# Gather, running sum and matmul on one core: casts moved from ScalarE into the gathers, single-tile drains, and an unrolled TensorE program

## The chip, the core and the metric

The kernel runs on one core of one Trainium2 chip. The metric is the device time of one execution in microseconds (us). Executions were timed in rounds, each kernel beside the kernel before on the same chip. "TensorE", "VectorE", "ScalarE" and "GpSimd" stand in the profile as PE (with PEld for the loading of weights), DVE, ACT and POOL; SP is SyncE, which here only issues loads and stores.

## The reference

```python
B, S, N, D = 16, 4096, 2048, 512
# x: (16, 4096, 512) f32; indices: (16, 2048) int64, sorted, no repeats; w: (512, 512) f32
gathered = x[np.arange(B)[:, None], indices, :]
out = np.matmul(np.cumsum(gathered, axis=1), w)        # (16, 2048, 512) f32
```

32,768 rows of 2 KB are fetched (67 MB) and as many rows of 2 KB are written (67 MB). The kernel works in 256 tiles of 128 rows. Two tiles make a group.

## The kernel before

For every tile GpSimd issues one indirect DMA that fetches 128 rows of f32. ScalarE casts a group to fp16. TensorE multiplies the tile with a triangular matrix, which gives the running sums inside the tile, already transposed (L149, `pa`). VectorE adds the last column of the tile before and writes fp16 (`cst`). TensorE multiplies with `w` (L185, `pb`). ScalarE copies the product of a group out of PSUM in one go, and SyncE stores it.

```python
def gather(t):                       # GpSimd
    g, r = divmod(t, R)              # R = 2 tiles in a group
    if g >= NG // R:                 # NG = 16 tiles in flight
        pool.need(s_c0, R)
        pool.need(s_c, g - NG // R)  # buffer free when the cast of 8 groups ago is done
    ...
    nc.gpsimd.indirect_dma_start(out=g32[g % (NG // R)][:, r, :], in_=x_flat, ...)

def cast(g):                         # ScalarE, three groups ahead of its drain
    for t in range(R * g, R * g + R):
        act.need(s_g[t % NG], 16 * (t // NG + 1))
    act.need(s_a, R * (g - NH + 1))
    nc.scalar.copy(out=g16[g % NH][:], in_=g32[g % (NG // R)][:]).then_inc(s_c, 1)

def drain(g):                        # ScalarE
    act.need(s_o[g % NO], 16 * (g // NO))
    act.need(s_b, R * (g + 1))
    nc.scalar.copy(out=ob[g % NO][:], in_=pb[g % NB][:]).then_inc(s_e, 1)
...
# TensorE: the middle of its program is a loop whose waits compare with a register
with nc.tensor.Fori(LOOP, G - LOOP, LOOP) as first:
    for g in range(LOOP):
        step(g, first)               # project(g, j), then sums of two groups ahead
```

Of the kernel before, what the change touches and what calls it, by code (L numbers as in the profile page):

```python
# [7 lines left out]
P = 128  # L8
FP32 = mybir.dt.float32
FP16 = mybir.dt.float16  # L10
# [17 lines left out]
def kernel(  # L28
# [7 lines left out]
    nc = tc.nc  # L36

    B, S, D = x.shape
    N = indices.shape[1]
    R = 2  # L40
    Q = P // R
    DC = D // P
    NT = N // P
    T = B * NT
    G = T // R
# [1 line left out]
    KI = T // P  # L47
    FIRST = 2 * R
    NG = 16
    NH = 4  # L50
    NA = 4
    NB = 2
    NC = 4
    NO = 8
    LOOP = 4
    AH = 2
    assert D == 512 and N % (R * P) == 0 and T % P == 0

# [2 lines left out]
    const = ctx.enter_context(tc.tile_pool(name="const", bufs=1))  # L61
    ps = ctx.enter_context(tc.tile_pool(name="ps", bufs=1, space=bass.MemoryType.PSUM))
# [3 lines left out]
    idxf = const.tile([P, KI, P], FP32)  # L66
    idxg = const.tile([P, KI, P], U32)
# [3 lines left out]
    ident = const.tile([P, P], FP32)  # L71
    zeros = const.tile([P, D], FP16)
    spare = const.tile([P, 1], FP16)
    g32 = [const.tile([P, R, D], FP32, name=f"g32_{i}") for i in range(NG // R)]
    g16 = [const.tile([P, R, D], FP16, name=f"g16_{i}") for i in range(NH)]
    cst = [const.tile([P, DC, R, P], FP16, name=f"cst{i}") for i in range(NC)]
    ob = [const.tile([P, R, D], FP32, name=f"ob{i}") for i in range(NO)]
    pa = [ps.tile([P, DC, R, Q], FP32, name=f"pa{i}") for i in range(NA)]
    pb = [ps.tile([P, R, D], FP32, name=f"pb{i}") for i in range(NB)]

    ctx.enter_context(tc.tile_critical(no_gpsimd_drain=True))  # L81

    def sem(name):
        return tc.alloc_semaphore(name)

    s_z, s_ut, s_wc, s_if, s_pt, s_prep, s_c0, s_c1 = (
        sem(f"s_{n}") for n in ("z", "ut", "wc", "if", "pt", "prep", "c0", "c1")
    )
# [3 lines left out]
    s_el = [sem(f"s_el{j}") for j in range(R)]  # L92
    s_ol = [sem(f"s_ol{j}") for j in range(R)]
    s_g = [sem(f"s_g{i}") for i in range(NG)]
    s_o = [sem(f"s_o{i}") for i in range(NO)]
    s_c = sem("s_c")
    s_a = sem("s_a")
    s_d = sem("s_d")
    s_b = sem("s_b")
    s_e = sem("s_e")  # L100

    pool, pe, dve, act, sp = (
        Lane(e) for e in (nc.gpsimd, nc.tensor, nc.vector, nc.scalar, nc.sync)
    )

    def gather(t):
        g, r = divmod(t, R)
        if g >= NG // R:
            pool.need(s_c0, R)
            pool.need(s_c, g - NG // R)  # L110
        if t < FIRST:
            pool.need(s_first[g], 16)
            ap = idx_first[:, t, 0:1]
        else:
            pool.need(s_prep, t // P + 1)
            ap = idxg[:, t // P, t % P : t % P + 1]
        nc.gpsimd.indirect_dma_start(  # L117
            out=g32[g % (NG // R)][:, r, :],
            out_offset=None,
            in_=x_flat,  # L120
            in_offset=bass.IndirectOffsetOnAxis(ap=ap, axis=0),
            element_offset=(t // NT) * S * D,
        ).then_inc(s_g[t % NG], 16)

    def cast(g):
        for t in range(R * g, R * g + R):
            act.need(s_g[t % NG], 16 * (t // NG + 1))
        act.need(s_a, R * (g - NH + 1))
        nc.scalar.copy(out=g16[g % NH][:], in_=g32[g % (NG // R)][:]).then_inc(s_c, 1)  # L129

    def cast_tile(t, done):
        g, r = divmod(t, R)
        act.need(s_g[t % NG], 16 * (t // NG + 1))
        act.need(s_a, R * (g - NH + 1))
        nc.scalar.copy(out=g16[g % NH][:, r], in_=g32[g % (NG // R)][:, r]).then_inc(done, 1)  # L135

    def sums(t, first=0):
        g, r = divmod(t, R)
        if isinstance(first, int):
            if g in (0, G - 1):  # L140
                pe.need(s_c1 if g else s_c0, r + 1)
            else:
                pe.need(s_c, g)
            pe.need(s_ut, 4)
            pe.need(s_d, t - NA + 1)
        elif r == 0:
            nc.tensor.wait_ge(s_c, first + g)
        for c in range(DC):
            mm = nc.tensor.matmul(  # L149
                out=pa[t % NA][:, c],  # L150
                lhsT=g16[g % NH][:, r, c * P : (c + 1) * P],
                rhs=ut[:],
                start=(c == 0),
                stop=(c == DC - 1),
            )
        mm.then_inc(s_a, 1)

    def carry(t):
        g, r = divmod(t, R)
        dve.need(s_b, R * (g - NC + 1))  # L160
        dve.need(s_a, t + 1)
        dst = cst[g % NC][:, :, :, r * Q : (r + 1) * Q]
        if t % NT == 0:
            nc.vector.tensor_copy(out=dst, in_=pa[t % NA][:]).then_inc(s_d, 1)  # L164
            return
        e = (r - 1) % R
        last = cst[(t - 1) // R % NC][:, :, R - 1, e * Q + Q - 1 : e * Q + Q]
        dve.need(s_d, t)
        nc.vector.tensor_tensor(  # L169
            out=dst,  # L170
            in0=pa[t % NA][:],
            in1=last.unsqueeze(2).broadcast_to([P, DC, R, Q]),
            op=mybir.AluOpType.add,
        ).then_inc(s_d, 1)

    def project(g, j, first=0):
        if isinstance(first, int):
            pe.need(s_wc, DC)
            pe.need(s_d, R * (g + 1))
            pe.need(s_e, g - NB + 1)  # L180
        elif j == 0:
            nc.tensor.wait_ge(s_d, R * first + R * (g + 1))
            nc.tensor.wait_ge(s_e, first + (g - NB + 1))
        for c in range(DC):
            mm = nc.tensor.matmul(  # L185
                out=pb[g % NB][:, j],
                lhsT=cst[g % NC][:, c, j, :],
                rhs=w16[:, c, :],
                start=(c == 0),
                stop=(c == DC - 1),  # L190
            )
        mm.then_inc(s_b, 1)

    def drain(g):
        act.need(s_o[g % NO], 16 * (g // NO))
        act.need(s_b, R * (g + 1))
        nc.scalar.copy(out=ob[g % NO][:], in_=pb[g % NB][:]).then_inc(s_e, 1)  # L197

    def store(g):
        b, h = divmod(g, GB)  # L200
        dst = out[b, h * R * P : (h + 1) * R * P, :].rearrange("(p j) d -> p j d", j=R)
        sp.need(s_e, g + 1)
        nc.sync.dma_start(out=dst, in_=ob[g % NO][:]).then_inc(s_o[g % NO], 16)

    def drain_last(j, lane, copy):
        g = G - 1
        lane.need(s_o[g % NO], 16 * (g // NO))
        lane.need(s_b, R * g + j + 1)
        copy(out=ob[g % NO][:, j], in_=pb[g % NB][:, j]).then_inc(s_el[j], 1)  # L209

    def store_last():
        b, h = divmod(G - 1, GB)
# [6 lines left out]
    with nc.allow_non_contiguous_dma(reason="a few indices, one per partition"):  # L219
        for k, eng in enumerate((nc.sync, nc.scalar)):  # L220
            t = k * R
            eng.dma_start(
                out=idx_first[:, t : t + R, :],
                in_=indices[0, t * P : (t + R) * P]
# [15 lines left out]
    for j in range(R):  # L240
# [7 lines left out]
        out=ident[:],  # L248
        in_=ident[:],
# [7 lines left out]
        out=ut[:],  # L257
# [12 lines left out]
    def busy(n):  # L270
        pe.need(s_z, 1)
        for _ in range(n):
            nc.tensor.matmul(  # L273
                out=pb[NB - 1][:, R - 1], lhsT=zeros[:, :P], rhs=zeros[:], start=True, stop=True
            )

    nc.vector.memset(zeros[:], 0.0).then_inc(s_z, 1)  # L277
# [4 lines left out]
    for k in range(KI):  # L282
        pe.need(s_ut, 3)
        pe.need(s_if, k + 1)
        nc.tensor.transpose(  # L285
            out=pb[k % NB][:, 0, :P], in_=idxf[:, k, :], identity=ident[:]
        ).then_inc(s_pt, 1)
    busy(10)
    for k in range(KI):
        dve.need(s_pt, k + 1)  # L290
        nc.vector.tensor_copy(out=idxg[:, k, :], in_=pb[k % NB][:, 0, :P]).then_inc(s_prep, 1)  # L291
    for c in range(DC // 2, DC):
        dve.need(s_w[c], 16)
        nc.vector.tensor_copy(out=w16[:, c, :], in_=w32[:, c, :]).then_inc(s_wc, 1)  # L294
# [2 lines left out]
    drain_last(0, dve, nc.vector.tensor_copy)  # L297


    def step(g, first=0):  # L300
        for j in range(R):
            project(g, j, first)
            if not isinstance(first, int) or g + AH < G:
                sums(R * (g + AH) + j, first)

    for t in range(R):
        sums(t)
    pe.need(s_prep, KI)
    for j in range(R):
        project(0, j)  # L310
        sums(R + j)
    for t in range(2 * R, R * (AH + 1)):
        sums(t)
    for g in range(1, LOOP):
        step(g)
    with nc.tensor.Fori(LOOP, G - LOOP, LOOP) as first:
        for g in range(LOOP):
            step(g, first)
    for g in range(G - LOOP, G - AH - 1):
        step(g)  # L320
    project(G - 3, 0)
    project(G - 3, 1)
    sums(T - 2)
# [9 lines left out]
    for c in range(DC // 2):  # L333
        act.need(s_w[c], 16)
        nc.scalar.copy(out=w16[:, c, :], in_=w32[:, c, :]).then_inc(s_wc, 1)  # L335
    for t in range(R):
        cast_tile(t, s_c0)
    for g in range(1, AH + 1):
        cast(g)
    for g in range(G - 1):  # L340
        if g + AH + 1 < G - 1:
            cast(g + AH + 1)
        elif g + AH + 1 == G - 1:
            for t in range(T - R, T):
                cast_tile(t, s_c1)
        drain(g)
    drain_last(1, act, nc.scalar.copy)

# [29 lines left out]
```

## Time and profile before

| | |
|---|---|
| time, median of 3 | 351.32 us (350.12 to 351.76) |
| span of the first profiled execution | 451.1 us |
| bytes moved by DMA | 135.66 MB |
| busy in that profile, TensorE / ScalarE / GpSimd / VectorE | 324 / 249 / 244 / 180 us |

The profile was 100 us longer than the timed runs.

How to read the page: part 2 cuts the span into 40 slices; a digit is the busy share of a slice in tenths; the row "GB/s" is what the DMA engines wrote or read in that slice, counted in the size of the packets' records. Part 3 has one line for each DMA queue: packets, MB, and the time that its packets took as a share of 16 engines over the span. q0 carries the gathers, q1 the stores. Part 4 follows the work that ended last back to the start.

### The profile page before, as it was taken

To read this page: it belongs to the slowest core of one execution; us is meant where nothing else is said; L and a number is where in the kernel's file an instruction comes from. 1 tells how busy PE (TensorE), PEld (TensorE's weight loads), DVE (VectorE), ACT (ScalarE), POOL (GpSimd) and SP (SyncE) were. 2 spreads that over 40 slices of the span, in tenths; PEclk is the share of its full clock that TensorE was granted. 3 is DMA by queue.
4 is the path that set the end of the run, shared out by engine and by line. 5 is a ranking of instruction groups with operands and counts; after the bars stand their busy time and mean duration, and the time that the engine had idled before them with its cause. 6 is when DMAs were issued, how large, how long until landed. Compare 5 with 4: busy or idle time off the path is not lost.

```text
span 451.1 us, 6060 instructions
## 1 busy us (share of the span) xinstructions
PE 323.7 (72%) x2069; PEld 170.2 (38%) x2069; DVE 179.5 (40%) x264; ACT 249.4 (55%) x262; POOL 243.8 (54%) x264
## 2 busy tenths in 40 slices
PE   6236678767696966977679766777758776768795
PEld 2113344334343533443344333343334343334352
DVE  3103334434334444444324533444432443333662
ACT  3403546645556656656446745665554664545883
POOL 6773565555565755655565556655556555556300
PEclk9865997969979899889998999898999898899999
DMA  7774998888999999988998999888898888898875
GB/s 225 233 232 141 329 324 274 309 304 306 333 304 345 315 352 336 327 301 307 332 310 280 345 339 331 293 309 300 296 347 313 288 295 306 308 320 314 285 289 232
DMA packets 40476, 135.66 MB, mean 301 GB/s; under 512 B 6800, under 2 KB 7056, under 8 KB 40464
## 3 DMA queue, kind: packets, MB, share of 16 engines
q0 software_dynamic: 20480, 67.13, 48.2%
q1 hardware_dynamic: 19712, 68.43, 37.7%
q14 instruction: 11, 0.09, 0.1%
q10 hardware_dynamic: 272, 0.00, 0.0%
q8 instruction: 1, 0.02, 0.0%
HBM read 68.42 MB, written 67.11 MB: 300 GB/s over the span
## 4 chain that ended last, share of the span: by engine, by line
PE 64%; another core or an unknown queue 14%; DVE 8%; issue 6%; ACT 5%; DMA 2%; DVEq 1%; ACTq 0%; SPq 0%
PE pb L185 51%; PE pa L149 13%; DVE cst L169 8%; ACT ob L197 3%; ACT g L129 2%; DVEq L23 1%; DMA g<-in_x_dram,idx_first 1%; DVE cst L164 0%; DMA idx_first<-in_indices_dram 0%; ACT g L135 0%; ACT ob L209 0%; ACTq L23 0%; SPq L373 0%; SPq L81 0%
## 5 line engine op out<-in xcount | busy, mean ns | idle before, releaser
L185 PE MATMUL pb<-w,cst 128*128 128x512 f16 x1024 | 288.4, 408 | 118.5 <-DVE cst L169 75.8
L117 POOL DMA_INDIRECT g<-in_x_dram,idxg x252 | 238.7, 947 | 178.4 <-ACT g L129 103.9
L169 DVE TENSOR_TENSOR cst<-pa,cst 128x512 f16<-128x512 f32 x240 | 166.0, 692 | 237.9 <-PE pa L149 135.5
L197 ACT COPY ob<-pb 128x1024 f32<-128x1024 f32 x127 | 128.8, 1014 | 186.1 <-PE pb L185 140.5
L185 PEld LDWEIGHTS pb<-w,cst 128*128 128x128 f16 x1024 | 93.4, 104 | 199.4 <-DVE cst L169 57.0
L129 ACT CAST g<-g 128x1024 f16<-128x1024 f32 x126 | 132.4, 1051 | 4.1 <-DMA g<-in_x_dram,idxg 2.8
L149 PEld LDWEIGHTS pa<-ut,g 128*128 128x128 f16 x1024 | 82.5, 102 | 71.0 <-issue 15.7
L149 PE MATMUL pa<-ut,g 128*128 128x128 f16 x1024 | 104.3, 227 | 2.4 <-ACT g L135 1.4
L164 DVE CAST cst<-pa 128x512 f16<-128x512 f32 x16 | 11.0, 686 | 20.1 <-PE pb L185 10.3
L273 PE MATMUL pb<-zeros 128*128 128x512 f16 x19 | 6.4, 503 | 1.5 <-DVE zeros L277 1.5
L117 POOL DMA_INDIRECT g<-in_x_dram,idx_first x4 | 4.0, 996 | 2.3 <-DMA idx_first<-in_indices_dram 1.4
L273 PEld LDWEIGHTS pb<-zeros 128*128 128x128 f16 x19 | 2.3, 125 | 4.4 <-issue 1.9
L135 ACT CAST g<-g 128x512 f16<-128x512 f32 x4 | 2.4, 619 | 1.9 <-DMA g<-in_x_dram,idx_first 1.6
L335 ACT CAST w<-w 128x512 f16<-128x512 f32 x2 | 1.2, 618 | 3.0 <-DMA w<-in_w_dram 3.0
L332 ACT ACT_TABLE_LOAD x1 | 1.3, 1283 | 1.5 <-SPq L81 1.5
L294 DVE CAST w<-w 128x512 f16<-128x512 f32 x2 | 1.1, 552 | 2.4 <-DMA w<-in_w_dram 2.4
L280 DVE CAST idxf<-idx 128x128 f32<-128x128 uint32 x2 | 0.6, 288 | 2.8 <-DMA idx<-in_indices_dram 2.8
L209 DVE COPY ob<-pb 128x512 f32<-128x512 f32 x1 | 0.7, 692 | 1.2 <-PE pb L185 1.2
L209 ACT COPY ob<-pb 128x512 f32<-128x512 f32 x1 | 0.6, 586 | 0.8 <-PE pb L185 0.8
L291 DVE CAST idxg<-pb 128x128 uint32<-128x128 f32 x2 | 0.5, 290 | 0.9 <-PE pb L285 0.9
L277 DVE MEMSET zeros<- 128x256 uint32 x1 | 0.3, 272 | 1.1 <-SPq L81 1.1
L285 PEld LDWEIGHTS pb<-ident,idxf 128*128 128x128 f32 x2 | 0.5, 231 | 0.5 <-issue 0.5
(10 smaller groups left out, 2.2 us busy)
## 6 DMA issues: line engine op xcount, KB each, us to landing
out_dram<-ob SPq DMA_DIRECT2D x127, 512.0 KB
g<-in_x_dram,idxg POOLq DMA_INDIRECT x252
w<-in_w_dram SPq DMA_DIRECT2D x4, 256.0 KB
out_dram<-ob SPq DMA_DIRECT2D x2, 256.0 KB, 2.7
idx<-in_indices_dram SPq DMA_DIRECT2D x2, 128.0 KB, 2.7
g<-in_x_dram,idx_first POOLq DMA_INDIRECT x4
idx_first<-in_indices_dram ACTq DMA_DIRECT2D x1, 2.0 KB, 1.9
idx_first<-in_indices_dram SPq DMA_DIRECT2D x1, 2.0 KB, 2.1
```

The source lines that it names most:

```text
L23: self.eng.wait_ge(sem, value)
L117: nc.gpsimd.indirect_dma_start(out=g32[g % (NG // R)][:, r, :], out_offset=None, in_=x_flat, in_offset=bass.IndirectOffsetOnAxis(ap=ap, ax ...
L129: nc.scalar.copy(out=g16[g % NH][:], in_=g32[g % (NG // R)][:]).then_inc(s_c, 1)
L135: nc.scalar.copy(out=g16[g % NH][:, r], in_=g32[g % (NG // R)][:, r]).then_inc(done, 1)
L149: mm = nc.tensor.matmul(out=pa[t % NA][:, c], lhsT=g16[g % NH][:, r, c * P : (c + 1) * P], rhs=ut[:], start=(c == 0), stop=(c == DC - 1),)
L164: nc.vector.tensor_copy(out=dst, in_=pa[t % NA][:]).then_inc(s_d, 1)
L169: nc.vector.tensor_tensor(out=dst, in0=pa[t % NA][:], in1=last.unsqueeze(2).broadcast_to([P, DC, R, Q]), op=mybir.AluOpType.add,).then_inc ...
L185: mm = nc.tensor.matmul(out=pb[g % NB][:, j], lhsT=cst[g % NC][:, c, j, :], rhs=w16[:, c, :], start=(c == 0), stop=(c == DC - 1),)
L197: nc.scalar.copy(out=ob[g % NO][:], in_=pb[g % NB][:]).then_inc(s_e, 1)
L209: copy(out=ob[g % NO][:, j], in_=pb[g % NB][:, j]).then_inc(s_el[j], 1)
L273: nc.tensor.matmul(out=pb[NB - 1][:, R - 1], lhsT=zeros[:, :P], rhs=zeros[:], start=True, stop=True)
L332: nc.scalar.copy(out=spare[:], in_=zeros[:, :1])
```

## The change

The intent: the gathers, which GpSimd issues, convert on the way, so ScalarE need not cast, the gathers write half as many bytes into SBUF, and the way from a landed row to its sums is one engine shorter. With ScalarE free, products are drained tile by tile from four PSUM buffers, and TensorE's program is written out, so that its waits compare with constants. Smaller parts, not shown: five fewer warm-up matmuls, and TensorE's waits go by tile instead of by group. The core of the diff, with cuts marked by `...` and some comments added:

```diff
-    g32 = [const.tile([P, R, D], FP32, name=f"g32_{i}") for i in range(NG // R)]
-    g16 = [const.tile([P, R, D], FP16, name=f"g16_{i}") for i in range(NH)]
+    g16 = [const.tile([P, R, D], FP16, name=f"g16_{i}") for i in range(NG // R)]
...
-    pb = [ps.tile([P, R, D], FP32, name=f"pb{i}") for i in range(NB)]     # NB = 2
+    pb = [ps.tile([P, D], FP32, name=f"pb{i}") for i in range(NB)]        # NB = 4
...
     def gather(t):
-        if g >= NG // R:
-            pool.need(s_c0, R)
-            pool.need(s_c, g - NG // R)
+        pool.need(s_a, R * (g + 1) - NG)          # buffer free when summed
         nc.gpsimd.indirect_dma_start(
-            out=g32[g % (NG // R)][:, r, :],
+            out=g16[g % (NG // R)][:, r, :],      # f32 rows of x into fp16: the DMA converts
...
-    def cast(g):
...
+    def sums(t):
+        pe.need(s_g[t % NG], 16 * (t // NG + 1))  # TensorE waits for the gather itself
+        pe.need(s_d, t - NA + 1)
...
     def drain(g):
-        act.need(s_o[g % NO], 16 * (g // NO))
-        act.need(s_b, R * (g + 1))
-        nc.scalar.copy(out=ob[g % NO][:], in_=pb[g % NB][:]).then_inc(s_e, 1)
+        for j in range(R):
+            u = R * g + j
+            act.need(s_b, u + 1)
+            nc.scalar.copy(out=ob[g % NO][:, j], in_=pb[u % NB][:]).then_inc(s_e, 1)
...
-    with nc.tensor.Fori(LOOP, G - LOOP, LOOP) as first:
...
+    for g in range(1, G - AH - 1):
+        for j in range(R):
+            sums(R * (g + AH) + j)
+            project(g, j)
```

More of the change, by code (lines that the diff above doesn't have):

```diff
@@ L49 @@
     NG = 16
-    NH = 4
     NA = 4
-    NB = 2
+    NB = 4
     NC = 4
     NO = 8
-    LOOP = 4
     AH = 2
@@ L95 @@
     s_o = [sem(f"s_o{i}") for i in range(NO)]
-    s_c = sem("s_c")
     s_a = sem("s_a")
@@ L123, in gather @@
         ).then_inc(s_g[t % NG], 16)
-    def cast(g):
-        for t in range(R * g, R * g + R):
-            act.need(s_g[t % NG], 16 * (t // NG + 1))
-        act.need(s_a, R * (g - NH + 1))
-        nc.scalar.copy(out=g16[g % NH][:], in_=g32[g % (NG // R)][:]).then_inc(s_c, 1)
-    def cast_tile(t, done):
-        g, r = divmod(t, R)
-        act.need(s_g[t % NG], 16 * (t // NG + 1))
-        act.need(s_a, R * (g - NH + 1))
-        nc.scalar.copy(out=g16[g % NH][:, r], in_=g32[g % (NG // R)][:, r]).then_inc(done, 1)
-    def sums(t, first=0):
-        g, r = divmod(t, R)
-        if isinstance(first, int):
-            if g in (0, G - 1):
-                pe.need(s_c1 if g else s_c0, r + 1)
-            else:
-                pe.need(s_c, g)
-            pe.need(s_ut, 4)
-            pe.need(s_d, t - NA + 1)
-        elif r == 0:
-            nc.tensor.wait_ge(s_c, first + g)
+    def sums(t):
+        g, r = divmod(t, R)
+        pe.need(s_g[t % NG], 16 * (t // NG + 1))
+        pe.need(s_d, t - NA + 1)
         for c in range(DC):
+            if c == 1:
+                pe.need(s_e, t - R * AH - NB + 1)
             mm = nc.tensor.matmul(
                 out=pa[t % NA][:, c],
-                lhsT=g16[g % NH][:, r, c * P : (c + 1) * P],
+                lhsT=g16[g % (NG // R)][:, r, c * P : (c + 1) * P],
                 rhs=ut[:],
@@ L159, in carry @@
         g, r = divmod(t, R)
-        dve.need(s_b, R * (g - NC + 1))
         dve.need(s_a, t + 1)
@@ L174, in carry, with project @@
         ).then_inc(s_d, 1)
-    def project(g, j, first=0):
-        if isinstance(first, int):
-            pe.need(s_wc, DC)
-            pe.need(s_d, R * (g + 1))
-            pe.need(s_e, g - NB + 1)
-        elif j == 0:
-            nc.tensor.wait_ge(s_d, R * first + R * (g + 1))
-            nc.tensor.wait_ge(s_e, first + (g - NB + 1))
+    def project(g, j):
+        u = R * g + j
+        pe.need(s_e, u - NB + 1)
+        pe.need(s_d, min(R * (g + 1) + j, T))
         for c in range(DC):
             mm = nc.tensor.matmul(
-                out=pb[g % NB][:, j],
+                out=pb[u % NB][:],
                 lhsT=cst[g % NC][:, c, j, :],
@@ L194, in drain @@
     def drain(g):
-        act.need(s_o[g % NO], 16 * (g // NO))
-        act.need(s_b, R * (g + 1))
-        nc.scalar.copy(out=ob[g % NO][:], in_=pb[g % NB][:]).then_inc(s_e, 1)
+        for j in range(R):
+            u = R * g + j
+            act.need(s_b, u + 1)
+            nc.scalar.copy(out=ob[g % NO][:, j], in_=pb[u % NB][:]).then_inc(s_e, 1)
     def store(g):
@@ L201, in store @@
         dst = out[b, h * R * P : (h + 1) * R * P, :].rearrange("(p j) d -> p j d", j=R)
-        sp.need(s_e, g + 1)
+        sp.need(s_e, R * (g + 1))
         nc.sync.dma_start(out=dst, in_=ob[g % NO][:]).then_inc(s_o[g % NO], 16)
@@ L208, in drain_last @@
         lane.need(s_b, R * g + j + 1)
-        copy(out=ob[g % NO][:, j], in_=pb[g % NB][:, j]).then_inc(s_el[j], 1)
+        copy(out=ob[g % NO][:, j], in_=pb[(R * g + j) % NB][:]).then_inc(s_el[j], 1)
     def store_last():
@@ L273, in busy @@
             nc.tensor.matmul(
-                out=pb[NB - 1][:, R - 1], lhsT=zeros[:, :P], rhs=zeros[:], start=True, stop=True
+                out=pb[NB - 1][:], lhsT=zeros[:, :P], rhs=zeros[:], start=True, stop=True
             )
@@ L285 @@
         nc.tensor.transpose(
-            out=pb[k % NB][:, 0, :P], in_=idxf[:, k, :], identity=ident[:]
+            out=pb[k % NB][:, :P], in_=idxf[:, k, :], identity=ident[:]
         ).then_inc(s_pt, 1)
-    busy(10)
+    busy(5)
     for k in range(KI):
         dve.need(s_pt, k + 1)
-        nc.vector.tensor_copy(out=idxg[:, k, :], in_=pb[k % NB][:, 0, :P]).then_inc(s_prep, 1)
+        nc.vector.tensor_copy(out=idxg[:, k, :], in_=pb[k % NB][:, :P]).then_inc(s_prep, 1)
     for c in range(DC // 2, DC):
@@ L297 @@
     drain_last(0, dve, nc.vector.tensor_copy)
-    def step(g, first=0):
-        for j in range(R):
-            project(g, j, first)
-            if not isinstance(first, int) or g + AH < G:
-                sums(R * (g + AH) + j, first)
+    pe.need(s_ut, 4)
     for t in range(R):
@@ L308 @@
     pe.need(s_prep, KI)
+    pe.need(s_wc, DC)
     for j in range(R):
@@ L313 @@
         sums(t)
-    for g in range(1, LOOP):
-        step(g)
-    with nc.tensor.Fori(LOOP, G - LOOP, LOOP) as first:
-        for g in range(LOOP):
-            step(g, first)
-    for g in range(G - LOOP, G - AH - 1):
-        step(g)
+    for g in range(1, G - AH - 1):
+        for j in range(R):
+            sums(R * (g + AH) + j)
+            project(g, j)
     project(G - 3, 0)
@@ L335 @@
         nc.scalar.copy(out=w16[:, c, :], in_=w32[:, c, :]).then_inc(s_wc, 1)
-    for t in range(R):
-        cast_tile(t, s_c0)
-    for g in range(1, AH + 1):
-        cast(g)
     for g in range(G - 1):
-        if g + AH + 1 < G - 1:
-            cast(g + AH + 1)
-        elif g + AH + 1 == G - 1:
-            for t in range(T - R, T):
-                cast_tile(t, s_c1)
+        act.need(s_o[g % NO], 16 * (g // NO))
         drain(g)
```

## The prediction

> **What bounds the kernel now.** The first thing to read is the head of the page against the times: the profiled execution spanned 451.1 us, the three timed ones 350.12 to 351.76 us. So the profile shows the parts and their costs, but not the pace. I read the chain that ended last first, to see what the extra 100 us are.
>
> ```profile
> span 451.1 us, 6060 instructions
> PE 323.7 (72%) x2069; PEld 170.2 (38%) x2069; DVE 179.5 (40%) x264; ACT 249.4 (55%) x262; POOL 243.8 (54%) x264
> ...
> q0 software_dynamic: 20480, 67.13, 48.2%
> q1 hardware_dynamic: 19712, 68.43, 37.7%
> ...
> PE 64%; another core or an unknown queue 14%; DVE 8%; issue 6%; ACT 5%; DMA 2%; DVEq 1%; ACTq 0%; SPq 0%
> ```
>
> 14% "unknown queue" and 6% "issue" are some 90 us of 451 in which nothing that the profile knows was waited for; without them the chain is about 361 us. The timeline shows one such hole, in which VectorE sits 7.79 us before an addition (start, length, engine, what it does, idle before it and who ended that), although TensorE's four matmuls for it had started 8 us earlier:
>
> ```profile
> 13.65 0.39 PE L149 MATMUL pa<-ut,g 128*128 128x128 f16 x4
> ...
> 21.89 0.69 DVE L169 TENSOR_TENSOR cst<-pa,cst 128x512 f16<-128x512 f32 x1 [7.79 <-remote]
> ```
>
> I take these holes to belong to the profiled execution, and read floors instead: how long would each engine need alone for 256 tiles of 128 rows? The groups by line and the gathers' own view give the terms.
>
> ```profile
> L117 POOL DMA_INDIRECT g<-in_x_dram,idxg x252: 941/947/956, 8.6 to 424.4; - x126
> ...
>   ACT g L129: 103.9, 33
>   issue: 75.3, 222
> ```
>
> ```profile
> L185 PE MATMUL pb<-w,cst 128*128 128x512 f16 x1024 | 288.4, 408 | 118.5 <-DVE cst L169 75.8
> L117 POOL DMA_INDIRECT g<-in_x_dram,idxg x252 | 238.7, 947 | 178.4 <-ACT g L129 103.9
> L169 DVE TENSOR_TENSOR cst<-pa,cst 128x512 f16<-128x512 f32 x240 | 166.0, 692 | 237.9 <-PE pa L149 135.5
> L197 ACT COPY ob<-pb 128x1024 f32<-128x1024 f32 x127 | 128.8, 1014 | 186.1 <-PE pb L185 140.5
> L129 ACT CAST g<-g 128x1024 f16<-128x1024 f32 x126 | 132.4, 1051 | 4.1 <-DMA g<-in_x_dram,idxg 2.8
> ```
>
> **GpSimd (POOL)**: a gather takes 947 ns and 222 times the engine paused some 0.30 us before the next one without waiting for anybody. In the start times of the trace 201 of 255 intervals are under 1.35 us, with a mean of 1.252 us. Floor: 256 x 1.252 = 320.5 us, from the first gather at 3.4 us, so the last one cannot be issued before about 323 us.
> **DMA**: in the packet records a full packet of 4096 B has a median of 159 ns, on the gathers' queue (16,384 of them) and on the stores' (16,256). Floor of a tile: 64 + 64 such packets over 16 engines are 8 x 159 = 1.27 us, with the 9 ns completion packets about 1.29 us; 256 of them are some 330 us. The gathers' mean is 210 ns, because some take 579 ns, but with that mean the sum would be over 380 us, which the timed runs forbid. Check from the other side: 135.66 MB in 351.3 us are 386 GB/s on average, ramps included, about 400 without them; 16 engines at 4096 B per 159 ns are 412.
> **TensorE**: where nothing stops it, one tile (4 products and 4 sums) comes every 1.085 us (starts of L185 at 212.56, 213.65, 214.73 in the timeline): 278 us. **ScalarE**: a cast of 1051 ns and a drain of 1014 ns per two tiles: 264 us. **VectorE**: 177 us.
>
> So at full speed the DMA engines (1.29 us a tile) come first, gather issue (1.25) just behind, TensorE (1.09) and ScalarE (1.03) after that. In the first 17 us there are no stores, so half of the DMA engines' time is lost there: from then on 245 gathers and 256 stores at about 0.64 us each are 322 us, which ends at 339, plus some 3 us for the last landing: 342. The measured 351 is that plus some 9 us of small waits. My reading: **the kernel before runs at the DMA engines' pace, with gather issue 3% behind it**, and the rest is coupling: ScalarE does cast and drain in turn, a late gather delays the drain behind it, and POOL's real waits (103.9 us in 33 pieces) are all for a cast to free a buffer.
>
> [...] no transfer in this trace casts: this is the largest unknown.
> [...]
>
> **The change part by part.**
> *Converting gathers.* Removed: 126 casts of 1051 ns and 4 of 619 ns, 135 us of ScalarE. It was at 264 of 351 us, so off the bound, but it stood in the loop that frees gather buffers. A buffer is now freed when TensorE has summed it, a step later, but with the cast's 1.05 us and a semaphore gone from between; still 16 tiles can be in flight, 16 x 1.25 = 20 us, where the first gather needed about 5 us to land. So POOL should seldom wait. Gather count and descriptors stay: 320.5 us of issue stay. DMA: a row reads 2048 B as before and writes 1024 B instead of 2048. If a packet's time follows the bytes written, a tile costs 0.32 + 0.64 = 0.96 us and the DMA floor falls to 246 us; if it follows the bytes read, it stays at 1.29 us; if conversion has its own slower pace, it rises.
> *Single-tile drains.* 127 copies of 1014 ns become 254 of about 586 ns (the 128x512 copy of L209): 149 us, 20 more, on an engine that has just lost 135. It ends at some 150 of 340 us. Each bank comes free about 0.5 us earlier, and four banks as before hold four tiles.
> *Unrolled TensorE.* Removes branches and register waits: the holes before L185 that "issue" ended are 13.5 us in the profile, but TensorE is 70 us below the bound. No gain at the bound, some in the tail.
> *Start and end.* One cast of about 0.6 us and a semaphore leave the first and the last tile's path: 1 to 2 us.
>
> Sum for my main case: the DMA engines are relieved, gather issue takes over. Last issue at 3.4 + 255 x 1.252 = 322.7; 1 us for itself, about 4.5 us to land (the first gather: 3.4 to 8.8 us including its issue), some 5 tiles of TensorE left (5.4 us), drain and last store 3.5 us: 337 us. For small waits I add 1: **338 us**.
>
> **Rivals.**
> *A, the read side paces the packets.* Then DMA stays at 1.29 us a tile and only the coupling improves: 342 to 350 us. For it: nothing here says that a shorter write shortens a packet, and HBM still delivers every byte. Against it: the 579 ns packets are on the gathers' queue alone and may be writes held up.
> *B, the conversion is slower than a copy.* If a gather packet took twice 159 ns, a tile would cost 1.9 us, 490 us in all; at 1.3 times, 1.48 us, 380 to 390. For it: it is work that no packet of this trace does. Against it: the rest of the change (fewer warm-up matmuls, finer waits) looks like tuning around converting gathers that paid.
> *C, issue is faster without the profiler.* If the 0.30 us before a gather belongs to profiling, and the DMA is relieved, TensorE would be next: 278 us plus ramps, near 305 to 320. The timed runs before cannot tell, as DMA hid it.
> *D, gather issue grows with conversion,* to more than 947 ns: each 10 ns are 2.6 us.
>
> **Range and chances.** Main case (330 to 341) about half; A a quarter, part of it over 2% faster, that is under 344.3; B about 0.15; C about 0.1. Hence 338 with 324 to 360, faster 0.62, same 0.22, slower 0.16.
>
> **What would show it.** Right: gather starts 1.25 us apart almost throughout, with few waits on sums; ScalarE near 150 us busy with only drains; TensorE 1.085 us a tile in bursts with short holes that gathers end; DMA share clearly lower than 86%, shorter packets on q0. Wrong: q0 packets of 159 ns or longer for 1024 B rows, so that its share stays or grows (A, B); POOL waiting long on L126's sums because gathers land late (B); gather instructions longer than 947 ns (D).

A section of four points is cut from the recorded text but for a clause (the cuts are marked), because it rested on rules and figures that no trace or run of this case shows. The forecast's sum: 322.7 + 1 + 4.5 + 5.4 + 3.5 comes to 337 us, and with 1 us for small waits to 338. The first trace has two fetch records of 16 KB, of 1.3 and 1.9 us.

## The result

The changed kernel takes 356.7 us (median of 4, 356.05 to 357.03) against 351.5 us (median of 4). The ratio is 1.0154, with a 95% interval of 1.0123 to 1.0184. A ratio is the mean time of one kernel's fast runs over that of the other's fast runs of the same rounds, so it is not quite the ratio of the medians that are quoted. The prediction was 338.0 us: its range of 324 to 360 holds the result, but it forecast a gain of nearly 4%, and the change lost 1.5%.

The page of the kernel before, from a profile at its usual speed (span, then the DMA rows of part 2, the queues, the chain by engine, the groups of the gathers and of ScalarE, and the gathers' time from issue to landing):

```profile
span 351.9 us, 6060 instructions
...
DMA  7699999999999999999999999999999999999855
GB/s 233 205 280 351 347 407 408 416 418 414 416 415 419 414 417 414 415 416 414 416 415 415 414 412 414 406 415 413 410 414 413 414 415 415 412 415 413 336 215 217
...
q0 software_dynamic: 20480, 67.13, 49.0%
q1 hardware_dynamic: 19712, 68.43, 48.3%
...
POOL 51%; DMA 24%; issue 18%; ACT 2%; PE 2%; SPq 0%; ACTq 0%; POOLq 0%
...
L117 POOL DMA_INDIRECT g<-in_x_dram,idxg x252 | 238.4, 946 | 76.8 <-issue 72.2
...
L129 ACT CAST g<-g 128x1024 f16<-128x1024 f32 x126 | 131.7, 1045 | 81.9 <-issue 76.0
...
g<-in_x_dram,idxg POOLq DMA_INDIRECT x252, 11.6
```

The same rows of the page of the kernel after:

```profile
span 355.3 us, 5483 instructions
...
DMA  6899999999999999999999999999999999999986
GB/s 177 118 217 294 291 297 296 309 296 302 301 297 309 277 317 287 306 300 304 292 301 309 288 319 289 304 303 291 313 294 314 286 297 297 305 295 304 300 288 239
...
q0 software_dynamic: 36864, 33.57, 58.0%
q1 hardware_dynamic: 19712, 68.43, 51.1%
...
HBM read 68.42 MB, written 67.11 MB: 381 GB/s over the span
...
DMA 60%; POOL 24%; issue 9%; PE 5%; ACT 0%; SPq 0%; ACTq 0%
...
L111 POOL DMA_INDIRECT g<-in_x_dram,idxg x252 | 236.4, 938 | 83.2 <-issue 62.6
...
L170 ACT COPY ob<-pb 128x512 f32<-128x512 f32 x254 | 148.9, 586 | 193.7 <-PE pb L157 193.7
...
g<-in_x_dram,idxg POOLq DMA_INDIRECT x252, 16.2
```

Four things are to be seen.

- The casts are gone, and ScalarE's drains wait 193.7 us in all for products. That engine was relieved as intended. It bought some 2 us at the end of the run, as is seen below, and the gathers cost more than that.
- The row "GB/s" falls from some 415 to some 300, which looks like DMA engines with room to spare. It is not: the row "DMA" is 9 tenths in every slice but the first two and the last two. The GB/s count a converting packet with the 1 KB that it writes, and the engine's time does not follow that: such a packet took 96 ns, a plain one of 4 KB 159 ns (below).
- The gathers' queue carries half the bytes (33.57 instead of 67.13 MB) in more packets (36,864 instead of 20,480), and its share of the engines' time grows from 49.0 to 58.0%.
- A gather takes a median of 16.2 us from issue to landing, not 11.6. The chain of work that ended last went mostly through GpSimd before; now DMA is 60% of it.

The waits tell the same from GpSimd's side. First the kernel before, then the kernel after (engine, line, waited for whom: total us, times, longest us):

```profile
POOL g L117 <- issue: 73.1, 240, 0.3
...
POOL g L117 <- ACT g L129: 4.6, 15, 0.3
```

```profile
PEld pa L126 <- DMA g<-in_x_dram,idxg: 104.7, 161, 1.4
POOL g L111 <- issue: 63.5, 208, 0.3
...
POOL g L111 <- PE pa L126: 20.7, 47, 0.9
```

Before, GpSimd hardly ever waits for a buffer: it issues every 1.25 us, ahead of the DMA engines, until its gathers are all out at 322.6 us. After, all 16 tiles in flight are under way at times, and GpSimd waits 20.7 us for sums to free a buffer, because the sums wait for gathers to land (104.7 us of waits before their loads of weights). Its last gather goes out at 327.0 us.

The packet records of the two traces give the reason in numbers (median of a full packet, and the pace at which tiles pass VectorE):

| | kernel before | kernel after |
|---|---|---|
| gather packets | 16,384 of 4096 B (two rows), 159 ns | 32,768 of 1024 B written (one row), 96 ns |
| per row of 2 KB read | 79.5 ns | 96 ns |
| store packets of 4096 B | 159 ns | 172 ns |
| pace of a tile, 40 to 300 us | 1.278 us | 1.316 us |
| pace of a tile, tile 32 to tile 240 | 1.293 us | 1.318 us |

The first window flatters the kernel before: at 40 us it is catching up after a slow start (tiles 16 to 32 pass in 17.4 us, 1.09 us each). Counted by tiles the kernel after is 0.026 us slower per tile, some 6.6 us over 256 tiles. It lost 5.2, so a little was given back elsewhere; where, an experiment below shows. The medians alone would give far more: 8 rows for each engine at 16.5 ns more are 132 ns a tile. A packet's record says how long it was open, which need not be what it cost; this gap is taken up again below.

### The profile page after: what moved, and what is told of

Same layout as the page of the kernel before. It is cut to its first block, busy times and chain, and to the rows that moved or that the text cites. A ratio compares the mean times of both kernels' runs of the same rounds, so it can differ in the third digit from the quotient of the medians.

```text
span 355.3 us, 5483 instructions
## 1 busy us (share of the span) xinstructions
PE 309.4 (87%) x2064; PEld 150.3 (42%) x2064; DVE 180.3 (51%) x264; ACT 152.2 (43%) x259; POOL 241.5 (68%) x264
## 3 DMA queue, kind: packets, MB, share of 16 engines
q0 software_dynamic: 36864, 33.57, 58.0%
HBM read 68.42 MB, written 67.11 MB: 381 GB/s over the span
## 4 chain that ended last, share of the span: by engine, by line
DMA 60%; POOL 24%; issue 9%; PE 5%; ACT 0%; SPq 0%; ACTq 0%
DMA g<-in_x_dram,idxg 60%; POOL g L111 24%; PE pb L157 3%; PE pa L126 2%; DMA idx_first<-in_indices_dram 1%; ACT ob L182 0%; SPq L331 0%; ACTq L23 0%; SPq L78 0%
## 5 line engine op out<-in xcount | busy, mean ns | idle before, releaser
L157 PE MATMUL pb<-w,cst 128*128 128x512 f16 x1024 | 264.9, 382 | 2.0 <-DVE cst L145 2.0
L170 ACT COPY ob<-pb 128x512 f32<-128x512 f32 x254 | 148.9, 586 | 193.7 <-PE pb L157 193.7
L126 PE MATMUL pa<-ut,g 128*128 128x128 f16 x1024 | 101.3, 223 | 38.0 <-DMA g<-in_x_dram,idxg 34.2
L126 PEld LDWEIGHTS pa<-ut,g 128*128 128x128 f16 x1024 | 68.4, 99 | 130.6 <-DMA g<-in_x_dram,idxg 104.7
L157 PEld LDWEIGHTS pb<-w,cst 128*128 128x128 f16 x1024 | 90.1, 98 | 65.0 <-issue 3.1
L182 ACT COPY ob<-pb 128x512 f32<-128x512 f32 x1 | 0.6, 587 | 1.4 <-PE pb L157 1.4
## 6 DMA issues: line engine op xcount, KB each, us to landing
g<-in_x_dram,idxg POOLq DMA_INDIRECT x252, 16.2
```

The source lines that it names most:

```text
L126: mm = nc.tensor.matmul(out=pa[t % NA][:, c], lhsT=g16[g % (NG // R)][:, r, c * P : (c + 1) * P], rhs=ut[:], start=(c == 0), stop=(c == DC ...
L157: mm = nc.tensor.matmul(out=pb[u % NB][:], lhsT=cst[g % NC][:, c, j, :], rhs=w16[:, c, :], start=(c == 0), stop=(c == DC - 1),)
L170: nc.scalar.copy(out=ob[g % NO][:, j], in_=pb[u % NB][:]).then_inc(s_e, 1)
L182: copy(out=ob[g % NO][:, j], in_=pb[(R * g + j) % NB][:]).then_inc(s_el[j], 1)
```

## The experiments

**Theory 1**: the DMA engines set the pace of both kernels. A converting gather costs them more per row than a plain one, because each row is a packet of its own and the time follows the bytes read. **Theory 2**: a gathered byte costs the same either way, and the loss comes from the other parts (drains, TensorE's order, the written-out program). **Theory 3**: gather issue, or the later release of gather buffers, binds the kernel after.

### One part of the change at a time

**unroll_only**: the kernel before with TensorE's loop written out.

```diff
-    with nc.tensor.Fori(LOOP, G - LOOP, LOOP) as first:
-        for g in range(LOOP):
-            step(g, first)
-    for g in range(G - LOOP, G - AH - 1):
+    for g in range(LOOP, G - AH - 1):
         step(g)
```

> The kernel before with TensorE's loop written out, nothing else. Theory 1 (the DMA engines set the pace, and a converting gather costs them more per row: 96 ns packets of one row against 159 ns packets of two): TensorE is not the bound, so 350 to 353 us. Theory 2 (a gathered byte costs the same either way, and the 5 us come from the other parts of the change): if the unrolling is the part that costs, 355 to 358 us here.

Measured: 350.96 us, ratio 0.9992 (0.9951 to 1.0033). Writing the loop out costs and gains nothing.

**conv_unroll**: that kernel with converting gathers and without any cast; drains of two tiles and TensorE's order stay as before.

```diff
-    g32 = [const.tile([P, R, D], FP32, name=f"g32_{i}") for i in range(NG // R)]
-    g16 = [const.tile([P, R, D], FP16, name=f"g16_{i}") for i in range(NH)]
+    g16 = [const.tile([P, R, D], FP16, name=f"g16_{i}") for i in range(NG // R)]
...
-        if g >= NG // R:
-            pool.need(s_c0, R)
-            pool.need(s_c, g - NG // R)
+        pool.need(s_a, R * (g + 1) - NG)
...
-            out=g32[g % (NG // R)][:, r, :],
+            out=g16[g % (NG // R)][:, r, :],
...
-            if g in (0, G - 1):
-                pe.need(s_c1 if g else s_c0, r + 1)
-            else:
-                pe.need(s_c, g)
+            pe.need(s_g[t % NG], 16 * (t // NG + 1))
...
-            cast(g + AH + 1)
...
```

> The kernel before with the loop written out and converting gathers instead of ScalarE casts; two-tile drains and TensorE's order as before. Theory 1: 355 to 360 us, with one packet of about 96 ns per row on the gathers' queue. Theory 2 (conversion indifferent, single-tile drains or the new order cost): 350 to 352 us.

Measured: 355.61 us, ratio 1.0122 (1.0076 to 1.0168), with 32,768 gather packets of 96 ns and a pace of 1.316 us per tile between 40 and 300 us, as in the kernel after. Converting gathers alone bring nearly all of the loss: 4.65 us between these two kernels of the same rounds.

**rest_only**: the counterpart. It is the kernel after with plain gathers and the old casts on ScalarE, two tiles at a time. Its edit, some 40 lines that put these back, is left out here.

> The kernel after with plain gathers and the ScalarE casts of before put back (two tiles at a time, three groups ahead), so all parts of the change but the converting gathers; right result. Theory 1: the other parts do no harm, 345 to 352 us. Theory 2: 355 to 358 us, the loss stays without converting gathers.

Measured: 350.94 us, ratio 0.9993 (0.9952 to 1.0035). All parts but the conversion together leave the time where it was. Theory 2 falls.

**plain_no_cast**: the kernel after with the conversion undone in the gathers and nothing put in its place; the sums read a constant fp16 tile. The result is wrong. All waits stay.

```diff
-    g16 = [const.tile([P, R, D], FP16, name=f"g16_{i}") for i in range(NG // R)]
+    g32 = [const.tile([P, R, D], FP32, name=f"g32_{i}") for i in range(NG // R)]
...
-            out=g16[g % (NG // R)][:, r, :],
+            out=g32[g % (NG // R)][:, r, :],
...
-                lhsT=g16[g % (NG // R)][:, r, c * P : (c + 1) * P],
+                lhsT=ut[:].rearrange("p a b -> p (a b)"),
```

> The kernel after with the conversion alone undone in the gathers: f32 rows land in f32 buffers, nothing casts them, and the sums read a constant fp16 tile instead, so the result is wrong on purpose while all waits and counts stay. Theory 1: DMA packets go back to 159 ns for two rows, the tile's DMA cost falls from 1.32 to about 1.27 to 1.29 us, and the time to 342 to 349 us. Theory 2: 356 to 358 us, as the kernel after. Theory 3 (gather issue with late buffer release is the bound): also 356 to 358 us.

Measured: 349.05 us, ratio 0.9934 (0.9894 to 0.9974). The queues in its page, to be held against those of the kernel after above (packets, MB, share of the engines):

```profile
q0 software_dynamic: 20480, 67.13, 49.5%
q1 hardware_dynamic: 19712, 68.43, 49.0%
```

The gathers write twice the bytes of the kernel after and take less of the engines' time, 49.5 against 58.0%. With the same waits and the same release of buffers the time falls by 7.6 us against the 356.7 of the kernel after, and by 6.6 us against conv_unroll, which ran in the same rounds, so theory 3 falls too. The bytes that HBM delivers and takes are the same in all these kernels (68.42 and 67.11 MB before and after), so they are not what changed either. It also shows what a path without any cast is worth when the gather does not pay for it: 2.2 us against the kernel before of its rounds.

**before_again** gave the fast profile of the kernel before that is shown above.

> The kernel before, unchanged, for a profile that is not slowed as the first one was (451 us). Theory 1 (DMA bound): 350 to 353 us, DMA at 9 tenths and about 410 GB/s in every middle slice, packets of 159 ns on both queues, one tile every 1.28 to 1.30 us, GpSimd issuing every 1.25 us with hardly a wait for buffers.

Measured: 353.57 us (a single run, profiled), just over what was expected and 2.9 us over the median of the kernel before in the same rounds, 350.7; 159 ns on both queues, 1.278 us a tile between 40 and 300 us, 4.6 us of waits for buffers.

### Less work for the DMA engines

**after_no_store**: the kernel after with all stores but the last eight left out. Its output is wrong, which doesn't matter for the time.

```diff
-    for g in range(G - 1):
+    for g in range(G - NO, G - 1):
         store(g)
...
-        act.need(s_o[g % NO], 16 * (g // NO))
         drain(g)
...
```

> The kernel after with all stores but the last eight left out, wrong on purpose. Theory 1: gathers alone need 0.77 us of the DMA engines per tile, so the time falls until gather issue (1.245 us a tile, 318 us from 3.4 us on) binds: 331 to 337 us, gathers land within 6 us. Theory 3 (gather issue or late buffer release binds the kernel after): hardly any change, 352 to 357 us.

Measured: 338.23 us, ratio 0.9647 (0.9591 to 0.9702); its fastest run took 337.34 us, so the time lies just above the expected 331 to 337. Gathers start every 1.243 us without a stop. This is the time that the prediction named, 338: it is what the kernel would take if the DMA engines really had been relieved and gather issue had taken over.

**after_skip16**: every 16th store left out, 8 of 128. Its output is wrong, which doesn't matter for the time.

```diff
...
+        if g % NO == 3 and g // NO % 2:
+            return
         nc.sync.dma_start(out=dst, in_=ob[g % NO][:]).then_inc(s_o[g % NO], 16)
...
```

> The kernel after with every 16th store left out (8 of 128, wrong on purpose). Theory 1: a store of two tiles is 2 x 0.64 to 0.68 us of all 16 DMA engines, so 8 of them are 10 to 11 us less work and the time falls by nearly that, to 346 to 348 us. If the DMA engines were not the bound: 355 to 357 us.

Measured: 347.78 us, ratio 0.991 (0.9881 to 0.994), which is 8.6 us under the 356.35 that the kernel after took on the same chip (after_again, below). Sixteen tiles' stores at 0.64 us (4 packets x 159 ns on each engine, an estimate from the packet records) are 10.2 us of DMA work. Most of it comes off the time. So the DMA engines set the pace of the kernel after. No run takes DMA work from the kernel before in this way; there the share, the pace and the late landings speak for it.

The middle of the run, from 20 to 320 us, in the view of stretches: the kernel before, the kernel after, after_no_store and after_skip16, in that order. A line has, for each engine in the order of the heading, the busy time and in brackets the number of instructions; its last three numbers are TensorE's granted clock, the DMA share and GB/s:

```profile
core 0: us, PE busy (x) PEld busy (x) DVE busy (x) ACT busy (x) POOL busy (x), PEclk, DMA share, GB/s
20.00:320.00 300.00, 268.09 (x1840) 133.87 (x1837) 158.97 (x230) 224.16 (x230) 226.94 (x240) 0.99 1.02 408
```

```profile
20.00:320.00 300.00, 266.38 (x1824) 130.03 (x1823) 157.80 (x228) 134.10 (x229) 222.12 (x237) 1.00 1.13 298
```

```profile
20.00:320.00 300.00, 283.15 (x1931) 134.14 (x1929) 167.69 (x243) 141.62 (x243) 226.47 (x242) 1.00 0.84 109
```

```profile
20.00:320.00 300.00, 271.33 (x1881) 135.42 (x1880) 162.82 (x236) 137.50 (x235) 226.47 (x242) 1.00 1.14 295
```

The counts in brackets say how far each kernel got in the same 300 us: TensorE started 1840, 1824, 1931 and 1881 matmuls. The DMA share is 1.02 for the kernel before and 1.13 for the kernel after. A share over 1 means that packet records overlap. Counted from the records of these 300 us, the gathers' queue alone has more than 16 packets open at once, on 16 engines, in 22% of the time in the kernel after, in 23% with the stores gone, and in 0.2% in the kernel before: converting packets overlap with one another, and not only with the stores'. That is why the shares, and sums of packet times, overstate a converting gather, as is seen below.

### The disputed cost by itself

**cast_bench** is no kernel but a series of transfers, eight of each form with nothing beside them.

> No kernel but a measurement: eight transfers of each form with nothing beside them, plain and converting: gathers of rows of 256, 512 and 1024 f32 elements, GpSimd's direct loads of 512, 1024 and 2048 elements per partition, plain loads and stores of SyncE of 4 and 8 KB per partition. Wrong on purpose, as it computes nothing. If a converting packet costs by the bytes read plus a fixed part: 256 elements about 57 ns, 512 96 ns, 1024 about 176 ns, one row in each packet, and a plain gather of 256 element rows puts four rows in a packet of 159 ns. If conversion has its own slower rate per element: the time doubles with the width, 48, 96, 192 ns. Direct converting loads of 2048 elements then run at 10 to 20% under the plain ones' rate.

Measured, from the packet records (medians):

```
f32 elements of a row      256      512       1024      2048
read per row               1 KB     2 KB      4 KB      8 KB
converting: bytes of a packet (written)
                           512      1024      2048      4096     one row in each
converting: ns            60       98        173       324
plain: bytes of a packet  4096     4096      4096      8192     4, 2, 1 and 1 rows in each
plain: ns                 173      159       159       309
```

The widths 256, 512 and 1024 are gathers, 2048 a direct load by GpSimd. Direct loads of 512 and 1024 elements gave the same 98 and 173 ns converting and 159 ns plain. The converting row is a straight line: (324 - 60) / 7 KB are 37.7 ns per KB **read**, plus 22 ns for each packet. The plain packets give (309 - 159) / 4 KB, 37.5 ns per KB, plus 9 ns. The packet of four 1 KB rows lies 14 ns above that line. So conversion has no slower rate of its own, and the halved write saves nothing. From first packet to last, eight direct loads of 2048 elements took 20.7 us converting and 20.8 us plain, so the 10 to 20% of the other expectation are not there; at 1024 elements it was 12.1 against 11.4 us. (Bytes read and bytes written go in step in these transfers. That the read side counts, and not a write side at half rate, is inferred from the equal slopes.) What it costs is a fixed part that is 13 ns larger and that is paid for each row, where a plain gather of 2 KB rows pays it once for two. Per row that is 98 against 79.5 ns by the packet records. A stream of gathers beside stores pays only part of this difference, by the pace a fifth to a quarter (26 to 34 of 132 ns a tile, against the kernel before and rest_only from tile 32 to tile 240), and how the two parts share in it was not separated. By the records, the narrower the row, the worse: at 1 KB it is 60 against some 43 (173 / 4), at 4 KB 173 against 159.

### A version built on these findings

If the DMA engines are full in the middle and partly idle in the first 20 us (share 0.70 in the kernel before), converting gathers might pay just there. **hybrid**, an edit of the kernel after, uses plain gathers and casts, and converts only in groups 0, 1 and 127; besides, the first group is projected, drained and stored as early as it can be.

```diff
...
+    gc = {g: const.tile([P, R, D], FP16, name=f"gc{g}") for g in (0, 1, G - 1)}
...
-            out=g32[g % (NG // R)][:, r, :],
+            out=gc[g][:, r, :] if g in gc else g32[g % (NG // R)][:, r, :],
...
+        if g == 0:
+            for j in range(R):
+                sp.need(s_e, j + 1)
+                nc.sync.dma_start(out=dst[:, j], in_=ob[0][:, j]).then_inc(s_o[0], 16)
+            return
...
```

> Right result. Plain gathers and ScalarE casts everywhere but in the first two groups and the last one, where gathers convert, because there the DMA engines have time to spare and the cast lies on the path; besides, the first group's two products are made before the next sums, drained before the next cast and stored tile by tile, so that the first store starts some 3 us earlier. If the DMA engines' pace in the middle (1.28 to 1.29 us a tile, plain packets) and the unused DMA time of the ramps set the time: 347.5 to 350 us, 0.3 to 1% under the kernel before. If the ramps are not on the path: 350 to 352 us.

> The same kernel as hybrid once more: the chip of the first try ran even the kernel before in 452 to 465 us, so it said nothing about the ramps. On a chip that runs the kernel before in some 351 us: 347.5 to 350 us if the ramps are on the path, 350 to 352 us if not.

The first two tries landed on two chips on which the kernel before itself took 452 to 465 and 448 to 463 us. There hybrid took 441.27 and 440.95 us (ratios 0.9552, interval 0.9363 to 0.974, and 0.9659, 0.9501 to 0.9818). That is a different condition of the chip, and nothing is concluded from it about the ramps. What made hybrid 3 to 5% faster there was not studied.

> The hybrid kernel a third time, beside the kernel after on one chip. On a chip that runs the kernel before in some 351 us: 347.5 to 350 us if the DMA engines' unused time in the ramps is on the path, 350 to 352 us if not. On a chip of the other kind (before at some 460 us) about 440 us, as twice seen, which leaves the ramps open.

> The kernel after, unchanged. On a chip of the 351 us kind: 355.5 to 357.5 us, the DMA engines' pace again. On a chip of the other kind it tells whether converting gathers also lose there: if the DMA engines set the pace, over the kernel before; if late semaphores do, under it, since the cast's hand-over is gone.

On a chip of the usual kind hybrid takes 350.79 us, ratio 0.9981 (0.9956 to 1.0007), and the kernel after in the same rounds 356.35 us, ratio 1.0142 (1.0115 to 1.0169). hybrid is as fast as the kernel before, not faster. Its first store does start earlier, at 16.4 us instead of 19.7 in before_again and 19.3 in rest_only, but the last gather lands at 337.9 us, against 336.9 in rest_only, and the end does not move. That the idle DMA time at the start can be turned into time was only argued, and this run speaks against it. No version with a right result beats the kernel before by more than the noise.

### Where the time lies

From the records of one execution each: when the last gather was issued, when its last packet was done, and the end.

| | issued | landed | end | landing | tail |
|---|---|---|---|---|---|
| before_again | 322.6 | 339.5 | 351.9 | 16.9 | 12.4 |
| rest_only | 322.2 | 336.9 | 349.0 | 14.7 | 12.1 |
| plain_no_cast | 322.2 | 337.2 | 346.9 | 15.0 | 9.7 |
| after | 327.0 | 345.8 | 355.3 | 18.8 | 9.5 |
| after_no_store | 320.5 | 326.8 | 337.3 | 6.3 | 10.5 |

The two kernels with stores and without any cast have a tail that is 2.4 to 2.9 us shorter than the two with casts. This is what the change gained. conv_unroll, which still drains two tiles at a time, has a tail of 9.6 us as well, so the gain comes from the missing casts and not from the single-tile drains. Against it stand 4.4 us of later issue and 1.9 us of longer landing. The balance is 3.4 us in these two executions. It is under the 5.2 us of the timed medians mainly because before_again was 2.9 us slower than the median of its rounds.

## Why the prediction was wrong

- **The floors were right.** GpSimd 1.252 us a gather (measured 1.250), DMA 1.29 us a tile (1.285 to 1.293 from tile 32 to tile 240 in the four plain kernels with correct results), TensorE behind them. That the kernel before runs at the DMA engines' pace with gather issue 3% behind fits before_again: its chain runs along GpSimd for 51%, but its last gather lands 16.9 us after its issue, where 6.3 us suffice when the stores are gone.
- **The holes were put down to the profiled execution.** That is wrong. Profiled executions on other chips were as fast as the rest, and on two chips all 22 executions of the kernel before took 448 to 465 us, like the first profile. Two things in the record go with this condition: a granted clock of 0.87 to 0.91 instead of 0.97 to 1.00, and a mean of 206 to 211 ns for a plain 4096 B gather packet instead of 165 to 166, at the same median of 159. The 579 ns packets that were counted against rival A belong to it: over 400 ns took 1,313 of 16,384 gather packets in the first profile and 153 in before_again. So do the 103.9 us of waits for casts, taken for coupling, which are 4.6 us in before_again. The conclusion, to reason from floors and not from that chain, survived this by luck. Why those chips are slow was not studied.
- **The step that failed** is in the change part by part: "If a packet's time follows the bytes written, a tile costs 0.32 + 0.64 = 0.96 us", and the sum that took this as its main case. That is 40 ns of an engine for each row; the packet of a row took 96. Its time follows the bytes read. cast_bench has 37.7 ns per KB read and 22 ns for each packet, and the pace is 1.316 us a tile, not one set by gather issue. In the terms of that sum: the last issue came at 327.0 and not 322.7 us, issuing and landing it took 18.8 us and not 5.5, and the rest 9.5 us and not 8.9.
- **Rival A** (the read side paces) had the mechanism, with a size that was off. It left out that a converting gather puts one row in a packet, where a plain one puts two, and that each packet's fixed part is larger by the records. Its term "DMA stays at 1.29 us a tile" measured 1.316, and 342 to 350 us became 356.7. Without those two costs, plain_no_cast, it is 349.05, inside A's range.
- **Rival B** multiplied the packet's time. By the medians a gather packet grew by 96 / 79.5 = 1.21 per row, and adding it up, 8 x 96 + 4 x 159 + some 18 ns for completion packets, gives 1.42 us a tile, 364 us for 256 (with the 172 and 22 ns that store and completion packets show in that trace even 1.50). The pace was 1.316. The sum is too high because packets that convert overlap, with one another and with the stores' (DMA share 1.13 where plain packets have 1.02). How an engine does that stays open.
- **Rival C** (faster issue without the profiler) fell: with stores gone the unprofiled time is 338.23 us, which is what 1.243 us a gather and the ramps give. **Rival D** fell: a converting gather is issued in 938 ns, a plain one in 946.
- **ScalarE, drains, unrolling**: some 150 us were expected and 152 measured, with no effect at the bound, as said. With TensorE's program written out, the queue of instructions q8 has 16 packets (0.26 MB) in the page of unroll_only instead of 2 (0.03 MB) in that of before_again, and unroll_only is as fast as the kernel before (350.96 us, ratio 0.9992). "1 to 2 us" off start and end were 2 to 3 us in the tail.
- **The chances.** The argument that the rest of the change "looks like tuning around converting gathers that paid" is no evidence from a profile, and it moved the odds of B and A too low. In the profile there was nothing for the written side; both sides of the question should have had equal weight.

## What to carry to other kernels

Before moving a cast into a DMA, ask what the DMA engines are paced by. In these runs it is bytes read plus a fixed cost per packet (cast_bench: 37.7 ns per KB and 22 ns converting, 37.5 and 9 ns plain), with one row in each converting packet, so a converting gather of narrow rows is dearer than a plain one (by the records 60 against some 43 ns for a row of 1 KB). On chips of the usual kind no run here shows a case in which it pays: hybrid, which converted only where the DMA engines were thought to have slack (share 0.70 in the first 20 us of the kernel before), was as fast as the kernel before (350.79 us, ratio 0.9981). Look at the DMA share and the packet times, not at GB/s: the converting gathers made the GB/s fall from some 415 to some 300 while the engines were as full as before, at 9 tenths. But the records overstate what a converting packet costs (132 ns a tile, of which the pace shows 26 to 34), so the size of a loss has to be tried.
